# Retention without GpSimd steps, and a new order of the hybrid mixer's products, in a four-layer transformer kernel

## The chip, the core and the metric

One core of one Trainium2 chip runs the whole program. The metric is the device time of one execution in microseconds. Before the change it is 3003.79 us, the median of 3 runs (3002.36 to 3005.44).

## The reference

The input is 512 tokens of 1024 channels, in fp32. Four layers follow one another, each a mixer and a feed-forward part with residual additions: dilated attention with a short convolution, retention, and two hybrid layers. The change touches retention and the hybrid mixer, cut here to their core.

```python
def retention_mixer(xn, wq, wk, wv, wg, gn_gain, wo):      # 4 heads, q and k of 256, v of 512
    q, k, v = xn @ wq, (xn @ wk) * 256 ** -0.5, xn @ wv
    o = chunkwise_retention(rotary(q, pos), rotary(k, pos), v)
    mu, var = mean(o), mean((o - mu) ** 2)                  # over each head's 512 values
    o = (o - mu) * rsqrt(var + EPS) * gn_gain
    return (silu(xn @ wg) * o) @ wo

def hybrid_mixer(h, ...):                                   # 8 heads of 64
    q_nsa, kv_nsa, g_nsa, qkv_sb, g_merge = split(h @ w_in)
    # q is rotated; six kv parts: k and v for compressed, selected and window attention
    kc, vc = gelu(blocks(k) @ w1 + b1) @ w2, the same for v # compressed keys and values
    o_nsa = g0 * softmax(q kc) vc + g1 * softmax(q ks) vs + g2 * softmax(q kw) vw
    # stick breaking: weight of key j for query i is sigmoid(z_ij) * prod over j<l<i of (1 - sigmoid(z_il))
    g_a, g_b = split(sigmoid(g_merge))
    y = g_a * (o_nsa @ w_proj_nsa) + g_b * (o_sb @ w_proj_sb)
    return y @ w_out
```

With 512 tokens there are 8 blocks of 64 keys, and each query takes up to 16, so the selected branch sees all causal keys.

## The kernel before

All products run on TensorE in three parts (`mm3`, L161): weights and inputs are split into a rounded part and a remainder (`whi`, `wlo`; `xgh`, `xgl`), and three matmuls of them are summed. A weight unit of 512 KB is loaded by SyncE into `raw` (3 buffers), rounded by ScalarE into `whi` and subtracted by VectorE into `wlo` (4 buffers each; `unit`, L147 to L156). `lin_a` makes a product with channels on the partitions (24 matmuls of 512 columns a unit), `lin_b` one with tokens on the partitions, in four token blocks at once, and `lin_b_halves` the same by token halves: the first two blocks over all of the weights, a callback `done`, then the other two blocks. PSUM has eight banks under four names (`pa`, `psc`, `ptr`, `po`) with two buffers each.

The order that is written is a priority. The framework puts an instruction that is written later ahead of an earlier one on its engine, at build time, where it takes the earlier one to be waiting, and each engine then runs its list in order. So products that depend on little are put between the steps of a softmax. What such a product can't pass is its buffers: a `lin_a` product holds a `pa` bank until VectorE has moved it into an SBUF slot, and there are 76 slots of 128 x 512. `slot()` and `ring()` take slots from the head of a queue, and what is freed goes to its tail; a slot that is taken again is written only when its last reader is done.

Retention (`mix1`, L690): for each of four heads, `project` makes q and k and rotates them. VectorE multiplies by cosine and sine (L709, L710), GpSimd subtracts and adds (L711, L712), and `split` makes the two parts. Then come the values, the scores `weigh`, the gate, four output blocks `o` with their group norm (ScalarE writes `og`, L777; GpSimd multiplies by the gate, L778), the next head's `project`, the previous head's output product `out` (all of it in `pa` banks, added to `x` at L749), and the transposes of `og` into `gt` (L792). In the last head, `ssq_add` sums the squares of `x` on GpSimd (L297), and `ssq_col` (L305) reduces them with matmuls against a column of ones.

The hybrid mixer (`hyb`, L895) has these stages:
- **Entry.** The compressed and selected keys and values are made by `lin_b` (in the second hybrid layer, by token halves). `kv_branch` scales, rotates, packs and transposes the selected ones; then the same for the window keys (`w_in_c`) by `lin_b`; `compress` runs two small products with a gelu each; then q by `lin_b` and its rotation and transposes; then the second small products, and their results spread into `kz` and `vc` (L963 to L971); then the compressed scores and softmax (L974 to L1005).
- **Softmax stage.** For four head pairs and two branches: scores, softmax on VectorE and ScalarE (`softmax`, L487), and `finish`, which transposes the probabilities and multiplies by the values (`pv`).
- **Values and gates.** `tok_pack(w[2])` makes the stick-breaking values v and `gate` five gate tiles (`ga`, L1047).
- **Stick stage.** `heads` (L567) takes four head pairs: `prep` makes q and k of a pair by two `lin_a` products (`u`, L1065), `sticks` scores and scans (L510 to L520), and `merge_a` (L1070) multiplies a gate tile by its product; the fill list holds five of these.
- **After it.** The remaining gates, the second set of gates, and the output products.

Of the kernel before, what the change touches and what calls it, by code (L numbers as in the profile page):

```python
# [10 lines left out]
F32R = mybir.dt.float32r  # L11
# [58 lines left out]
class Kern:  # L70
# [148 lines left out]
    def lin_b_halves(self, w, xs, banks, done=None):  # L219
        cols = w.shape[2]  # L220
        per = UNIT // cols
        parts = [self.unit(w[:, k:k + per, :], UNIT) for k in range(0, KT, per)]
        outs = []
        for h in range(2):
            outs += [bank()[:, :cols] for bank in banks[2 * h:2 * h + 2]]
            for k in range(KT):
                wh, wl = parts[k // per]
                sl = slice(k % per * cols, k % per * cols + cols)
                for tb in (2 * h, 2 * h + 1):
                    tsl = slice(tb * 128, tb * 128 + 128)  # L230
# [459 lines left out]
    def mix1(self, nxt):  # L690
# [7 lines left out]
        def project(h):  # L698
            rot = []
            for w in (a["ret_wq"], a["ret_wk"]):  # L700
                t = [tmp.get(name="rt") for _ in range(4)]
                for e in range(2):
                    ps = self.lin_a(w, 2 * h + e, xs, self.pa())
                    if self.pending is not None:
                        self.norm()
                        nc.vector.tensor_tensor(cr, cr, self.rb, ALU.mult)
                        nc.vector.tensor_tensor(sr, sr, self.rb, ALU.mult)
                        self.free(self.rb)
                    nc.vector.tensor_tensor(t[2 * e], ps, cr, ALU.mult)  # L709
                    nc.vector.tensor_tensor(t[2 * e + 1], ps, sr, ALU.mult)  # L710
                nc.gpsimd.tensor_tensor(t[0], t[0], t[3], ALU.subtract)  # L711
                nc.gpsimd.tensor_tensor(t[1], t[1], t[2], ALU.add)  # L712
                rot.append([self.split(t[0], name="r0"), self.split(t[1], name="r1")])
            return rot

        def weigh(h, rot):
# [23 lines left out]
        def out(h, gt):  # L740
            nonlocal st
            for n in range(0, KT, 2):
                wh, wl = self.unit(a["ret_wo"][h, n // 2], UNIT)
                for e in range(2):
                    ps = self.pa()
                    for c in range(4):
                        sl = slice((e * 4 + c) * 128, (e * 4 + c) * 128 + 128)
                        self.mm3(ps, (wh[:, sl], wl[:, sl]), gt[c], c == 0, c == 3)
                    nc.vector.tensor_tensor(self.x[n + e], ps, self.x[n + e], ALU.add)  # L749
                    if h == 3:  # L750
                        st = self.ssq_add(st, n + e, self.x[n + e])
                        nx.append(self.xg_tile(self.x[n + e], nxt, n + e))
            self.free(gt)

        rot = project(0)
        for h in range(4):
# [7 lines left out]
            for i in range(4):  # L764
                o = self.po()
                for j in range(i + 1):
                    sl = slice((i - j) * 128, (i - j) * 128 + 128)
                    self.mm3(o, tuple(z[:, sl] for z in at[j]), v[j], j == 0, j == i)
                bn = self.sm(6, "bn")
                nc.vector.bn_stats(bn, o)  # L770
                ag = self.sm(2, "ag")
                nc.vector.bn_aggr(ag, bn)
                r = self.rstd(ag[:, 1:2], 1, 1.0)
                nb = self.sm(1, "nb")
                nc.vector.scalar_tensor_tensor(nb, ag[:, 0:1], -1.0, r, ALU.mult, ALU.mult)
                t = ro.get(name="og")
                nc.scalar.activation(t, o, AF.Identity, scale=r[:, 0:1], bias=nb[:, 0:1])  # L777
                nc.gpsimd.tensor_tensor(t, t, gs[i], ALU.mult)  # L778
                og.append(t)
            self.free(box, v, gs)  # L780
            if h < 3:
# [113 lines left out]
    def hyb(self, l, post, nxt):  # L895
# [20 lines left out]
        self.free(cmpt)  # L916


        def kv_branch(ps, name):
            ktok = [self.slot(name="kt") for _ in range(2)]  # L920
            vp = [self.slot(512, F32R, "vp") for _ in range(2)]
            for tb in range(4):
                rc = self.rc[:, tb:tb + 1]
                nc.scalar.activation(b2(ktok[tb // 2])[:, tb % 2, 0:128], ps[tb][:, 0:128], AF.Identity, scale=rc)
                self.pack(vp[tb // 2][:, tb % 2 * 256:tb % 2 * 256 + 256], ps[tb][:, 128:256], rc)
            for b in range(2):
                self.rope(b2(ktok[b])[:, :, 128:256], b2(ktok[b])[:, :, 0:128], 2 * b, 2, 2, rf)
            k = self.stack_k(self.slot, self.transp(ktok, 128), name)
            self.free(ktok)
            return k, vp  # L930

        kvs = [kv_branch([p[:, 256:512] for p in pkv], "ks")]
        ps = self.lin_b(a["w_in_c"][l], xs, [self.po, self.po, self.pa, self.pa])
        gates = self.small.tile([128, 96], F32, tag="gates", name=self.nm("gates"), bufs=1)
        for tb in range(4):
            nc.scalar.activation(gates[:, tb * 24:tb * 24 + 24], ps[tb][:, 256:280], AF.Sigmoid, scale=self.rc[:, tb:tb + 1])
        kvs.append(kv_branch(ps, "kw"))
        gk, w2k = self.compress(gbk, "ck", l)
        gv, w2v = self.compress(gbv, "cv", l)

        qt = []
        for tb, p in enumerate(self.lin_b(w[0], xs, [self.psc, self.psc, self.po, self.po])):
            raw = rf.get(name="qraw")
            nc.vector.tensor_scalar(raw, p, self.rc[:, tb:tb + 1], None, ALU.mult)
            qt.append(self.slot(name="qtok"))
            self.rope(qt[tb][:, None, :], raw[:, None, :], tb, 1, 8, rf)
        qs = [self.stack_q(self.slot, self.transp(qt, p * 128), 0.125, "q") for p in range(4)]
        self.free(qt)

        pk = self.psc()  # L950
        gv4 = rf.get(256, name="gv4")
# [12 lines left out]
        for j in range(4):  # L964
# [5 lines left out]
            r, c = slice(32 * j, 32 * j + 32), j % 2 * 256  # L970
            self.pack(vc[j // 2][r, c:c + 256], pvc[r, 0:128])  # L971

        cadd, cmul = self.table("cmp_add"), self.table("cmp_mul")
        pcT = []  # L974
        for kv in range(2):
# [5 lines left out]
                self.mm(st, kz[2 + kv][:, c], q, False, j == 3)  # L981
            sT = rf.get(name="sT")
            nc.scalar.copy(sT, st)
            s = self.ptr()
            for i in range(4):
                nc.tensor.transpose(s[:, i * 128:i * 128 + 128], sT[:, i * 128:i * 128 + 128], self.ident)
# [16 lines left out]
            for i in range(4):  # L1003
                nc.tensor.transpose(p[:, i * 128:i * 128 + 128], pc[:, i * 128:i * 128 + 128], self.ident)
            pcT.append(self.split(p, name="pcT"))  # L1005
        self.free(cadd, cmul, *kz)
        rp = self.ring(10)
        tas = [self.slot(name="ga") for _ in range(3)]
        onsa = []
        work = []  # L1010

# [13 lines left out]
        for j in range(4):  # L1025
            for b in range(2):
                ps = self.box(rp)
                for kv in range(2):
                    h = kv * 4 + j
                    self.softmax(qs[j], kvs[b][0], kv, causal, ps[kv],  # L1030
                                 gates.rearrange("p (i c) -> p i c", i=4)[:, :, h * 3 + 1 + b])
                if work:
                    finish(*work.pop())
                work.append((j, b, ps))
            self.free(qs[j])
        finish(*work.pop())
# [1 line left out]
        rp.close(), rt.close(), rc.close()  # L1038

        rf.close()  # L1040
        wm = a["w_in_a"][l]
        self.first_stick = None
        self.tok_pack(w[2], [self.pa, self.pa], v)

        def gate(g, n):
            ps = self.lin_a(wm, n, xs, self.pa())
            nc.vector.tensor_tensor(g, ps, self.rb, ALU.mult)  # L1047
# [22 lines left out]
        def merge_a(n):  # L1070
# [4 lines left out]
        ready = len(tas)  # L1075
        osb = self.heads(prep, lambda c, e, ps: self.sticks(c[0], c[1], e, ps, tmp),
                         v, rp, rt, rc, [lambda n=n: merge_a(n) for n in range(ready)])
        rp.close(), rt.close(), rq.close(), tmp.close(), ru.close(), rc.close()

        for n in range(ready, KT):  # L1080
            tas.append(self.slot(name="ga"))
            gate(tas[n], 8 + n)
            merge_a(n)
        self.free(onsa)
        gbs = []
        for n in range(KT):
            gbs.append(self.slot(name="gb"))
            gate(gbs[n], 16 + n)
            sigmoid(gbs[n])
        self.free(self.xs, self.rb)  # L1090
        ys = []
# [177 lines left out]
```

## Time and profile before

| | us |
|---|---|
| median of 3 runs | 3003.79 |
| profiled execution, its own time | 3006.11 |
| its span, from the first to the last instruction | 3004.4 |
| outside the span | 1.7 |
| TensorE matmuls busy | 2938.6 (98%) |
| VectorE busy | 1898.5 (63%) |
| ScalarE busy | 1362.9 (45%) |
| GpSimd busy | 280.8 (9%) |
| mean granted TensorE clock | 0.995 |

TensorE is busy for nearly all of the span, so the table is read by what is missing: 65.8 us in which no matmul ran, and the stretches in which the granted clock was at its lower level. Stages are read from windows of the trace, and what ended a wait from the view of waits.

### The profile page before, as it was taken

The numbers are of one execution on the slowest core, as the hardware profiler recorded it, in microseconds if no ns is written. First come the engines' busy times: TensorE is split into PE (matmuls) and PEld (weight loads), VectorE is DVE, ScalarE is ACT, GpSimd is POOL, SyncE is SP. The second block draws the span as 40 slices with busy tenths as digits, with TensorE's granted clock in tenths as the row PEclk, the third lists the DMA queues.
The fourth block names the chain that finished last, engine by engine and source line by source line (L and its number), as shares of the span: only waits on it lengthen the run. The fifth ranks groups of instructions, "written<-read, shape, count | busy, mean of one in ns | idle before, by whom it ended". The sixth has DMA issues, their size and how long they took to land.

```text
span 3004.4 us, 36799 instructions
## 1 busy us (share of the span) xinstructions
PE 2938.6 (98%) x14060; PEld 2432.1 (81%) x14060; DVE 1898.5 (63%) x3084; ACT 1362.9 (45%) x2268; POOL 280.8 (9%) x303
## 2 busy tenths in 40 slices
PE   8999999999999999999999999999999999999998
PEld 7788888888888788888787788888877878888887
DVE  6876774344544677535888648774279884587732
ACT  4834443333333444324567435443356673454432
POOL 1010000111110100011003011000120040110000
PEclk9999999999999999999999999999999999999999
DMA  4033333322222233333101332323241113333332
GB/s 160 29 107 97 99 96 92 111 88 83 82 87 80 89 96 95 99 116 126 45 32 53 104 107 85 98 93 96 90 142 43 36 53 102 99 99 98 96 92 73
DMA packets 83937, 267.91 MB, mean 89 GB/s; under 512 B 9776, under 2 KB 12464, under 8 KB 83760
## 3 DMA queue, kind: packets, MB, share of 16 engines
q1 hardware_dynamic: 83760, 265.55, 28.0%
q8 instruction: 111, 1.82, 0.2%
q14 instruction: 66, 0.54, 0.1%
HBM read 258.17 MB, written 6.29 MB: 88 GB/s over the span
## 4 chain that ended last, share of the span: by engine, by line
PE 87%; DVE 7%; ACT 3%; issue 1%; POOL 0%; DMA 0%; SPq 0%; DVEq 0%; ACTq 0%; POOLq 0%
PE pa L159 38%; PE psc L159 21%; PE po L159 15%; PE ptr L159 11%; PE ptr L536 1%; DVE om L519 1%; DVE xgl L271 1%; DVE p L520 1%; DVE ptl L268 0%; ACT p L496 0%; DVE wlo L155 0%; ACT whi L154 0%; DVE x L409 0%; DVE m L408 0%; DVE rp L847 0%
## 5 line engine op out<-in xcount | busy, mean ns | idle before, releaser
L155 DVE TENSOR_TENSOR wlo<-raw,whi 128x1024 fp32r<-128x1024 f32 (+3 forms) x497 | 587.6, 1184 | 484.2 <-ACT whi L154 479.9
L154 ACT CAST whi<-raw 128x1024 fp32r<-128x1024 f32 (+2 forms) x491 | 494.5, 1008 | 871.8 <-PE pa L159 354.9
L159 PE MATMUL pa<-xgh,whi 128*128 128x512 f32 (+1 forms) x1344 | 519.4, 386 | 0.0
L159 PE MATMUL pa<-xgl,whi 128*128 128x512 f32 (+1 forms) x1344 | 519.4, 386 | 0.0
L159 PE MATMUL pa<-xgh,wlo 128*128 128x512 f32 (+1 forms) x1344 | 519.1, 386 | 0.0
L297 POOL TENSOR_TENSOR acc<-acc,sq 128x512 f32<-128x512 f32 (+1 forms) x99 | 131.2, 1326 | 1747.3 <-ACT sq L295 1746.1
L159 PEld LDWEIGHTS pa<-xgh,whi 128*128 128x128 f32 x1344 | 252.9, 188 | 47.1 <-DVE rt L710 0.2
L159 PEld LDWEIGHTS pa<-xgh,wlo 128*128 128x128 f32 x1344 | 252.8, 188 | 46.7
L159 PEld LDWEIGHTS pa<-xgl,whi 128*128 128x128 f32 x1344 | 252.8, 188 | 46.2
L159 PE MATMUL psc<-xgl,whi 128*128 128x512 f32 x672 | 261.8, 390 | 1.0 <-DVE xgl L271 1.0
L159 PE MATMUL psc<-xgh,whi 128*128 128x512 f32 x672 | 262.0, 390 | 0.3 <-ACT xgh L270 0.3
L159 PE MATMUL psc<-xgh,wlo 128*128 128x512 f32 x672 | 261.3, 389 | 0.0
L267 ACT CAST hh<-y 128x512 fp32r<-128x512 f32 x88 | 54.6, 620 | 222.2 <-DVE y L370 222.2
L159 PEld LDWEIGHTS psc<-xgl,whi 128*128 128x128 f32 x672 | 126.2, 188 | 27.2 <-DVE xgl L271 1.3
L159 PEld LDWEIGHTS psc<-xgh,whi 128*128 128x128 f32 x672 | 126.2, 188 | 26.6 <-ACT xgh L270 0.7
L159 PEld LDWEIGHTS psc<-xgh,wlo 128*128 128x128 f32 x672 | 126.2, 188 | 26.1
L159 PE MATMUL ptr<-hh,whi 128*128 128x512 f32 x352 | 136.9, 389 | 0.0
L159 PE MATMUL ptr<-hl,whi 128*128 128x512 f32 x352 | 136.9, 389 | 0.0
L159 PE MATMUL ptr<-hh,wlo 128*128 128x512 f32 x352 | 136.9, 389 | 0.0
L344 DVE SCALAR_TENSOR_TENSOR y<-u,cols,y 128x510 f32<-128x510 f32 x176 | 131.7, 749 | 5.7
L343 DVE SCALAR_TENSOR_TENSOR y<-u,cols,y 128x511 f32<-128x511 f32 x176 | 131.1, 745 | 4.6 <-ACT y L340 4.1
L159 PE MATMUL po<-hh,wlo 128*128 128x512 f32 (+1 forms) x352 | 132.3, 376 | 0.0
(399 smaller groups left out, 5771.9 us busy)
## 6 DMA issues: line engine op xcount, KB each, us to landing
raw<-ffn_w_up SPq DMA_DIRECT2D x88, 512.0 KB, 3.5
raw<-w_up SPq DMA_DIRECT2D x88, 512.0 KB, 3.5
raw<-w_in_a SPq DMA_DIRECT2D x48, 512.0 KB, 3.5
raw<-ffn_w_down SPq DMA_DIRECT2D x32, 512.0 KB, 3.5
raw<-w_down SPq DMA_DIRECT2D x32, 512.0 KB, 3.5
raw<-w_in_b SPq DMA_DIRECT2D x24, 512.0 KB, 3.4
raw<-ret_wv SPq DMA_DIRECT2D x16, 512.0 KB, 3.4
raw<-ret_wg SPq DMA_DIRECT2D x16, 512.0 KB, 3.4
```

What stands on the lines that cost most here:

```text
L154: (nc.vector.tensor_copy if step < n else nc.scalar.copy)(hi[:, cs], raw[:, cs])
L155: nc.vector.tensor_tensor(lo[:, cs], raw[:, cs], hi[:, cs].bitcast(F32), ALU.subtract)
L159: self.nc.tensor.matmul(out, l, r, start=start, stop=stop)
L267: nc.scalar.copy(hi, src)
L271: nc.vector.scalar_tensor_tensor(lo, src, scale, hi.bitcast(F32), ALU.mult, ALU.subtract)
L297: nc.gpsimd.tensor_tensor(st["sum"][0][:, hs], st["sum"][0][:, hs], sq[:, hs], ALU.add)
L343: nc.vector.scalar_tensor_tensor(y[:, 1:T], u[:, 0:T - 1], self.col(w, i * 3 + 1), y[:, 1:T], ALU.mult, ALU.add)
L344: nc.vector.scalar_tensor_tensor(y[:, 2:T], u[:, 0:T - 2], self.col(w, i * 3), y[:, 2:T], ALU.mult, ALU.add)
L519: nc.vector.tensor_tensor_scan(r, r, r, 1.0, ALU.mult, ALU.min)
L520: nc.vector.tensor_tensor(be[:, :n - 1], be[:, :n - 1], om[:, 1:n], ALU.mult)
L536: nc.tensor.transpose(t[:, c:c + 128], ps[e][i][:, j * 128:j * 128 + 128], self.ident)
```

## The change

In retention, the rotation's subtract and add go to VectorE, each followed by its split. In `out`, every other product goes to a `psc` bank. The squares of the last two tiles of `x` are no longer added on GpSimd, but are reduced by `ssq_col` as tiles of their own. The group norm scales the gate by 1/sd on ScalarE and forms (o - mean) * gate on VectorE, from PSUM, in one step.

In the hybrid mixer, the window keys and q are made by token halves; the transposes of the selected keys move behind both gelus and those of the window keys behind the compressed scores; q moves behind `kz` and `vc`; gate tiles 8, 9 and 10 are made in the entry (behind the gelus, behind q, and inside the compressed scores). `finish` comes after the first of two softmaxes of a step. The values v and gates 11 and 12 become the first fill of the stick stage, behind the first stick scores, and the fifth merge moves behind that stage.

```diff
@@ lin_b_halves
-        parts = [self.unit(w[:, k:k + per, :], UNIT) for k in range(0, KT, per)]
+        parts = [self.unit(w[:, k:min(k + per, KT), :], min(per, KT - k) * cols) for k in range(0, KT, per)]
@@ mix1: project
-                nc.gpsimd.tensor_tensor(t[0], t[0], t[3], ALU.subtract)
-                nc.gpsimd.tensor_tensor(t[1], t[1], t[2], ALU.add)
-                rot.append([self.split(t[0], name="r0"), self.split(t[1], name="r1")])
+                r = []
+                for e, op in enumerate((ALU.subtract, ALU.add)):
+                    nc.vector.tensor_tensor(t[e], t[e], t[3 - e], op)
+                    r.append(self.split(t[e], name=f"r{e}"))
+                rot.append(r)
@@ mix1: out
-                    ps = self.pa()
+                    ps = (self.pa, self.psc)[e]()
-                        st = self.ssq_add(st, n + e, self.x[n + e])
+                        st = self.ssq_add(st, n + e, self.x[n + e], 2)
@@ mix1: group norm
-                nb = self.sm(1, "nb")
-                nc.vector.scalar_tensor_tensor(nb, ag[:, 0:1], -1.0, r, ALU.mult, ALU.mult)
-                nc.scalar.activation(t, o, AF.Identity, scale=r[:, 0:1], bias=nb[:, 0:1])
-                nc.gpsimd.tensor_tensor(t, t, gs[i], ALU.mult)
+                nc.scalar.activation(gs[i], gs[i], AF.Identity, scale=r[:, 0:1])
+                nc.vector.scalar_tensor_tensor(t, o, ag[:, 0:1], gs[i], ALU.subtract, ALU.mult)
@@ hyb: entry
-        kvs = [kv_branch([p[:, 256:512] for p in pkv], "ks")]
-        ps = self.lin_b(a["w_in_c"][l], xs, [self.po, self.po, self.pa, self.pa])
+        for h in range(2):
+            kv_branch(0, h, [p[:, 256:512] for p in pkv[2 * h:2 * h + 2]])
+        def kw_done(h, ps):
+            kv_branch(1, h, ps)
+            for tb, p in enumerate(ps, 2 * h):
+                nc.scalar.activation(gates[:, tb * 24:tb * 24 + 24], p[:, 256:280], AF.Sigmoid, scale=self.rc[:, tb:tb + 1])
+        self.lin_b_halves(a["w_in_c"][l], xs, [self.po, self.po, self.pa, self.pa], kw_done)
         gk, w2k = self.compress(gbk, "ck", l)
         gv, w2v = self.compress(gbv, "cv", l)
-        qt = []
-        for tb, p in enumerate(self.lin_b(w[0], xs, [self.psc, self.psc, self.po, self.po])):
...
+        kvs = [kv_stack(0, "ks")]
+        tas = []
+        def gate(n):
+            g = self.slot(name="ga" if n < 16 else "gb")
+            ps = self.lin_a(wm, n, xs, self.pa())
+            nc.vector.tensor_tensor(g, ps, self.rb, ALU.mult)
+            return g
+        tas.append(gate(8))
...
+        self.lin_b_halves(w[0], xs, [self.psc, self.psc, self.po, self.po], q_done)
+        tas.append(gate(9))
+        qs = [self.stack_q(self.slot, self.transp(qt, p * 128), 0.125, "q") for p in range(4)]
...
             nc.scalar.copy(sT, st)
+            if kv == 0:
+                tas.append(gate(10))
...
+        kvs.append(kv_stack(1, "kw"))
         rp = self.ring(10)
-        tas = [self.slot(name="ga") for _ in range(3)]
@@ hyb: softmax stage
...
-                if work:
-                    finish(*work.pop())
+                    if work:
+                        finish(*work.pop())
@@ hyb: values, gates, sticks
-        self.tok_pack(w[2], [self.pa, self.pa], v)
-        tas.extend(self.slot(name="ga") for _ in range(2))
-        for n, g in enumerate(tas):
-            gate(g, 8 + n)
+        def values():
+            self.tok_pack(w[2], [self.pa, self.pa], v)
+            tas.extend(gate(n) for n in (11, 12))
-                         v, rp, rt, rc, [lambda n=n: merge_a(n) for n in range(ready)])
+                         v, rp, rt, rc, [values] + [lambda n=n: merge_a(n) for n in range(ready - 1)])
         rp.close(), rt.close(), rq.close(), tmp.close(), ru.close(), rc.close()
+        merge_a(ready - 1)
```

## Rows read from the trace of the kernel before

**Rows 1.** The page, part 1: engine, busy us, share of the span, instructions

```profile
PE 2938.6 (98%) x14060; PEld 2432.1 (81%) x14060; DVE 1898.5 (63%) x3084; ACT 1362.9 (45%) x2268; POOL 280.8 (9%) x303
```

**Rows 2.** Windows: stretch, length, PE, PEld, DVE, ACT, POOL busy, PEclk, DMA, GB/s

```profile
1389.00:1459.00 70.00, 64.69 (x378) 54.06 (x378) 49.87 (x119) 35.53 (x75) 11.04 (x15) 0.95 0.30 93
1459.00:1571.00 112.00, 109.61 (x611) 88.61 (x610) 100.48 (x305) 78.41 (x204) 2.60 (x2) 1.00 0.11 36
1571.00:1594.00 23.00, 23.00 (x107) 19.17 (x107) 14.01 (x20) 11.44 (x18) 0.00 (x0) 1.00 0.25 81
1594.00:1677.00 83.00, 75.49 (x375) 57.86 (x373) 76.90 (x125) 60.41 (x130) 32.72 (x64) 1.00 0.20 61
2203.00:2273.00 70.00, 63.49 (x385) 52.78 (x384) 50.70 (x118) 35.63 (x75) 12.00 (x15) 1.00 0.33 106
```

**Rows 3.** Waits of TensorE in retention, 600 to 1012 us: total us, times, longest

```profile
PE pa L159 <- DVE x L749: 2.7, 4, 1.0
PE ptr L792 <- DVE gtl L271: 2.5, 2, 1.9
PE psc L159 <- DVE xgl L271: 1.0, 1, 1.0
```

**Rows 4.** Windows in retention's first head

```profile
690.00:700.00 10.00, 8.09 (x42) 6.52 (x41) 7.05 (x8) 3.47 (x5) 3.52 (x2) 1.00 0.32 105
700.00:710.00 10.00, 10.00 (x42) 8.20 (x41) 2.99 (x4) 2.74 (x4) 0.00 (x0) 0.83 0.16 54
```

**Rows 5.** Groups of GpSimd in retention: count, busy us, mean ns, idle before

```profile
L778 POOL TENSOR_TENSOR og<-og,g 128x512 f32<-128x512 f32 x16 | 20.5, 1295 | 262.2 <-ACT og L777 185.0 <-PE pa L159 74.3 <-issue 2.9
L711 POOL TENSOR_TENSOR rt<-rt,rt 128x512 f32<-128x512 f32 x8 | 18.2, 2270 | 0.0
```

**Rows 6.** Groups of VectorE in retention: two subtractions of one form, 128x512

```profile
L268 DVE TENSOR_TENSOR r1l<-rt,r1h 128x512 fp32r<-128x512 f32 x6 | 10.6, 1773 | 0.0
L268 DVE TENSOR_TENSOR r0l<-rt,r0h 128x512 fp32r<-128x512 f32 x6 | 4.2, 692 | 0.8
```

**Rows 7.** Timeline of TensorE at retention's end: start us, us, instruction, count

```profile
1011.43 0.95 PE L159 MATMUL ptr<-one,acc 128*128 128x1 f32 x8
```

**Rows 8.** Waits of TensorE in the first hybrid entry, 1389 to 1458 us

```profile
PE psc L159 <- DVE vc L268: 3.2, 1, 3.2
PE ptr L447 <- POOL kt L845: 0.9, 1, 0.9
```

**Rows 9.** Timeline of TensorE behind the long wait of that entry

```profile
1452.15 5.46 PE L159 MATMUL psc<-q,kz 128*128 128x512 f32 x12 [3.15 <-DVE vc L268]
```

**Rows 10.** Waits of TensorE at the second hybrid layer's first product, 2178 to 2190

```profile
PE psc L159 <- DVE wlo L155: 0.7, 2, 0.4
```

**Rows 11.** Groups of VectorE in the first softmax stage that serve other products

```profile
L155 DVE TENSOR_TENSOR wlo<-raw,whi 128x1024 fp32r<-128x1024 f32 x8 | 9.8, 1219 | 0.0
L1047 DVE TENSOR_TENSOR ga<-pa,rb 128x512 f32<-128x512 f32 x4 | 2.7, 676 | 0.0
L271 DVE SCALAR_TENSOR_TENSOR vp<-pa,rc,vp 128x256 fp32r<-128x256 f32 x4 | 1.9, 471 | 0.0
```

**Rows 12.** Timeline of VectorE behind that stage: results of two neighbouring lin_a products

```profile
1577.07 0.69 DVE L1065 TENSOR_TENSOR u<-pa,rb 128x512 f32<-128x512 f32 x1 [1.40 <-PE pa L159]
1582.51 0.69 DVE L1065 TENSOR_TENSOR u<-pa,rb 128x512 f32<-128x512 f32 x1 [2.64 <-PE pa L159]
```

**Rows 13.** A window of the softmax stage between two filler products

```profile
1485.00:1490.00 5.00, 3.98 (x27) 3.44 (x28) 4.91 (x16) 3.31 (x10) 0.00 (x0) 1.00 0.01 3
```

**Rows 14.** Waits of TensorE in the first half of the stick stage

```profile
PE psc L159 <- ACT om L512: 3.5, 4, 1.5
PE po L159 <- DVE ptl L268: 0.9, 2, 0.7
```

**Rows 15.** A window of the stick stage

```profile
1615.00:1625.00 10.00, 7.32 (x35) 5.06 (x33) 9.69 (x18) 8.92 (x21) 4.92 (x10) 1.00 0.25 79
```

More of the change, by code (lines that the diff above doesn't have):

```diff
@@ L916, in hyb, with kv_branch @@
         self.free(cmpt)
[L919 to L922, printed above, removed]
+        ktok = [[self.slot(name="kt") for _ in range(2)] for _ in range(2)]
+        vps = [[self.slot(512, F32R, "vp") for _ in range(2)] for _ in range(2)]
+        def kv_branch(i, h, ps):
+            for tb, p in enumerate(ps, 2 * h):
                 rc = self.rc[:, tb:tb + 1]
[L924 to L930, printed above, removed]
@@ L932, in hyb @@
-        kvs = [kv_branch([p[:, 256:512] for p in pkv], "ks")]
-        ps = self.lin_b(a["w_in_c"][l], xs, [self.po, self.po, self.pa, self.pa])
-        gates = self.small.tile([128, 96], F32, tag="gates", name=self.nm("gates"), bufs=1)
-        for tb in range(4):
-            nc.scalar.activation(gates[:, tb * 24:tb * 24 + 24], ps[tb][:, 256:280], AF.Sigmoid, scale=self.rc[:, tb:tb + 1])
-        kvs.append(kv_branch(ps, "kw"))
+                nc.scalar.activation(b2(ktok[i][h])[:, tb % 2, 0:128], p[:, 0:128], AF.Identity, scale=rc)
@@ new lines, in kv_branch, with kv_stack @@
+                self.pack(vps[i][h][:, tb % 2 * 256:tb % 2 * 256 + 256], p[:, 128:256], rc)
+            self.rope(b2(ktok[i][h])[:, :, 128:256], b2(ktok[i][h])[:, :, 0:128], 2 * h, 2, 2, rf)
+        def kv_stack(i, name):
+            k = self.stack_k(self.slot, self.transp(ktok[i], 128), name)
+            self.free(ktok[i])
+            return k, vps[i]
+        for h in range(2):
+            kv_branch(0, h, [p[:, 256:512] for p in pkv[2 * h:2 * h + 2]])
+        gates = self.small.tile([128, 96], F32, tag="gates", name=self.nm("gates"), bufs=1)
@@ L938, in hyb @@
+        def kw_done(h, ps):
+            kv_branch(1, h, ps)
+            for tb, p in enumerate(ps, 2 * h):
+                nc.scalar.activation(gates[:, tb * 24:tb * 24 + 24], p[:, 256:280], AF.Sigmoid, scale=self.rc[:, tb:tb + 1])
+        self.lin_b_halves(a["w_in_c"][l], xs, [self.po, self.po, self.pa, self.pa], kw_done)
         gk, w2k = self.compress(gbk, "ck", l)
         gv, w2v = self.compress(gbv, "cv", l)
-        qt = []
-        for tb, p in enumerate(self.lin_b(w[0], xs, [self.psc, self.psc, self.po, self.po])):
[L943 to L946, printed above, removed]
@@ L947, in hyb @@
-        qs = [self.stack_q(self.slot, self.transp(qt, p * 128), 0.125, "q") for p in range(4)]
-        self.free(qt)
+        kvs = [kv_stack(0, "ks")]
+        wm = a["w_in_a"][l]
+        tas = []
[5 more added lines that the diff above has]
+        tas.append(gate(8))
         pk = self.psc()
@@ L971, in hyb, with q_done @@
             self.pack(vc[j // 2][r, c:c + 256], pvc[r, 0:128])
+        qt = []
+        def q_done(h, ps):
+            for tb, p in enumerate(ps, 2 * h):
+                raw = rf.get(name="qraw")
+                nc.vector.tensor_scalar(raw, p, self.rc[:, tb:tb + 1], None, ALU.mult)
+                qt.append(self.slot(name="qtok"))
+                self.rope(qt[tb][:, None, :], raw[:, None, :], tb, 1, 8, rf)
+        self.lin_b_halves(w[0], xs, [self.psc, self.psc, self.po, self.po], q_done)
+        tas.append(gate(9))
+        qs = [self.stack_q(self.slot, self.transp(qt, p * 128), 0.125, "q") for p in range(4)]
+        self.free(qt)
         cadd, cmul = self.table("cmp_add"), self.table("cmp_mul")
@@ L1040, in hyb @@
         rf.close()
-        wm = a["w_in_a"][l]
         self.first_stick = None
-        self.tok_pack(w[2], [self.pa, self.pa], v)
-        def gate(g, n):
-            ps = self.lin_a(wm, n, xs, self.pa())
-            nc.vector.tensor_tensor(g, ps, self.rb, ALU.mult)
         def sigmoid(g):
@@ L1073, in merge_a @@
             nc.vector.tensor_tensor(tas[n], ps, tas[n], ALU.mult)
-        ready = len(tas)
+        def values():
+            self.tok_pack(w[2], [self.pa, self.pa], v)
+            tas.extend(gate(n) for n in (11, 12))
+        ready = 5
         osb = self.heads(prep, lambda c, e, ps: self.sticks(c[0], c[1], e, ps, tmp),
-                         v, rp, rt, rc, [lambda n=n: merge_a(n) for n in range(ready)])
+                         v, rp, rt, rc, [values] + [lambda n=n: merge_a(n) for n in range(ready - 1)])
         rp.close(), rt.close(), rq.close(), tmp.close(), ru.close(), rc.close()
+        merge_a(ready - 1)
         for n in range(ready, KT):
-            tas.append(self.slot(name="ga"))
-            gate(tas[n], 8 + n)
+            tas.append(gate(8 + n))
             merge_a(n)
@@ L1086, in hyb @@
         for n in range(KT):
-            gbs.append(self.slot(name="gb"))
-            gate(gbs[n], 16 + n)
+            gbs.append(gate(16 + n))
             sigmoid(gbs[n])
```

## The prediction

> **What bounds the kernel.** I read the page's first part, then windows by stage, then the waits of each stage, then single instructions. TensorE is busy for 98% of the span [rows 1], and the change neither adds nor removes products, so it can gain only what TensorE loses now: idle time between matmuls, and matmuls run at the lower of its two clock levels. In the stretches that the change touches this is about 7 us in retention [rows 3, 4]; in the first hybrid layer 5.3 us in the entry, 2.4 in the softmax stage and 7.5 in the stick stage, and in the second layer's entry 6.5 (length less busy) [rows 2]. The second layer's other stages repeat the first's within 0.2 us. The reader should also see who is short of time beside TensorE: VectorE is busy for 100.5 of 112 us in the softmax stage and 76.9 of 83 in the stick stage, but for 14.0 of 23 between them and 49.9 of 70 in the entry [rows 2]. So the change moves TensorE work (gates, v) between stages in which VectorE is the second bound. The profiled execution took 3006.1 us, 2.3 above the median; a difference of 0.2%, or 6.0 us, is about what a measurement of this kernel can tell from no change.
>
> **Retention.** Four waits for `x`, 2.7 us, are for one of the two `pa` banks [rows 3]. With products alternating between `pa` and `psc` a bank is needed again only four products later: minus 2.7. Two waits for `gtl` cost 2.5 us, the long one 1.9 in the first head [rows 3, 4], and behind it the granted clock is 0.83 over 10 us, that is 3.4 us at 1.2 GHz, or 1.7 lost [rows 4]. Before it stands the rotation: GpSimd takes 2.27 us for one subtraction, and VectorE's `r1l` beside it 1.77 where the same form, `r0l`, takes 0.69 [rows 5, 6]. On VectorE the two combining steps cost 2 x 0.69, so the chain gets little shorter, but nothing is stretched. Of the 1.9 + 1.7 I take half: minus 1.8 (ends 0 and 3.6). At the end one wait for `xgl`, 1.0 us [rows 3], should go, as the last square sums no longer run beside it: minus 1.0. Against it, `ssq_col` reduces three tiles in place of one; eight of its records take 0.95 us on TensorE [rows 7], so two more sets cost plus 1.9. The group norm replaces a GpSimd step of 1.30 us [rows 5] by a VectorE step from PSUM; the nearest row for VectorE is 0.69, and the next head's projection stands behind it on TensorE. VectorE gains 16 + 16 such steps, some 22 us over four heads, but is busy for only 7.05 of 10 us even around the long wait [rows 4]. I cost both at nothing; if that cover failed, they would cost one such wait per head, 1 us each. Sum: **minus 3.6**.
>
> **Entry.** The longest wait, 3.2 us, is for `vc`: the spreading of the compressed keys holds both `psc` banks while the filler has run out [rows 8]. The twelve matmuls behind it take 5.46 us [rows 9], where 24 matmuls of that width take 5.44 (two neighbouring results are that far apart [rows 12]), so 2.7 us are lost at 1.2 GHz. In the second layer this stage shows a granted clock of 1.00 [rows 2], so nothing of that kind is there. The change puts q behind that spreading, with its second token half on `po` banks, and three gates of 5.44 us into the entry, where half of v (48 matmuls, 10.9 us) stood. The rotated keys' wait of 0.9 [rows 8] goes behind the gelus. I leave 0.9 us per layer, for the compressed softmax. First layer 5.3 - 0.9 + 2.7, second 6.5 - 0.9: **minus 12.7** (ends 0 and minus 14.5). The four weight units of q are now wanted within one half, 10.9 us; the one place that already works so shows 0.7 us of waits for `wlo` [rows 10], which I keep in the range, not in the sum. Weights, SyncE's loads and their number are the same, in another order: where six units fall together, with v and two gates behind the first sticks, they are wanted at one per 5.4 us, as between the stages now (81 GB/s [rows 2]).
>
> **Softmax stage.** This is the price. Now half of v and five gates (168 matmuls at 0.227 us, 38.1 us) fill it. Without them TensorE's own work is 109.6 - 38.1 = 71.5 us, and VectorE's 100.5 less `wlo`, `ga` and `vp` (9.8 + 2.7 + 1.9) [rows 11] = 86.1. What follows in the new order are the first `prep` products. By the queue of slots their results (`u`) take slots of the ring that the last `pv` of this stage still writes, so only two can run ahead, filling both `pa` banks and stopping every product behind them, v too. So TensorE has 71.5 + 10.9 = 82.4 us of work, and VectorE 86.1 + 4 x 1.22 for weights = 91.0. If VectorE is never idle, TensorE waits 8.6 us, against 2.4 now: plus 6.2, and 0.7 for moving the first `u` at the stage's end. For two layers **plus 13.8**. Ends: plus 2, if VectorE does part of this under the entry; plus 33, if the two products are used up in the entry and TensorE idles as in a slice with no filler, busy for 3.98 of 5 us [rows 13]: 71.5 / 0.796 = 89.8, so 18.3 idle, less 2.4, plus 0.7, twice.
>
> A rule speaks against this step by the clock. In the slice of the stick stage with most waits TensorE is busy for 7.32 of 10 us and its granted clock stays 1.00 [rows 15], so I give the clock no term. The Trainium skill (TensorE: Matmul & The Clock Gate, section on psum-queue depth-cycling) says that brief idling between groups of matmuls can make the clock go back and forth; by it the sum would lie higher, and the trace does not agree so far.
>
> **Stick stage.** The waits of its first half, 3.5 + 0.9 us [rows 14], come while the first sticks pile up on VectorE. With v and two gates behind the first scores (32.7 us of TensorE work, some 16 of VectorE's), VectorE has caught up before the next. I take 3.6 of 4.4 per layer: **minus 7.2** (ends 0 and minus 8.8). The later waits stay; the fifth merge behind the stage only moves. The new place of `finish` changes the order, not the work: nothing, as VectorE's sum bounds that stage either way.
>
> **The sum** is -3.6 - 12.7 + 13.8 - 7.2 = -9.7 us: 2996.4 against the profiled execution, 2994 against the median.
>
> **Rivals.**
> 1. Forecast, 2994 us, chance 0.36.
> 2. The starved stage costs next to nothing (plus 2 for both layers): -21.5, 2982 us. For it: VectorE has 20 us to spare in the entry. Against: the softmax steps can't start before q. Chance 0.16.
> 3. Slower: the softmax stage is starved in full, plus 33 and the other terms as forecast, +9.5, 3013 us. It decides where TensorE idles over 14 us there per layer (break-even); over 17 it is slower by 0.2%. For it: the slice without filler [rows 13]. Against: two products should be left for it. Chance 0.23.
> 4. The entry is not filled: q's halves wait for weights or for the banks as `vc` did, and that term is 0: +3.0, 3007 us, no change that can be told. Chance 0.18.
> 5. The clock falls in the starved stage. One fall costs 1.7 us [rows 4]; one per head pair, four a layer, gives +13.6 on the forecast: 3008 us. For it: both falls above came with a wait of 1.9 us or more. Against: rows 15. Chance 0.07. The rule of the skill above is this rival.
>
> **How the numbers follow.** Cases 1 and 2 lie under 2997.8 us, but case 1 only by 4 us, so 0.05 of it goes to no change: faster 0.47, same 0.05 + 0.18 + 0.07 = 0.30, slower 0.23. The range runs from case 2, with 2 us for a retention chain that goes entirely, to nearly case 3: 2980 to 3012. In this range the softmax stage's bounds and the 0.7 us waits for weights are held.
>
> **What would show it.** Right: no wait for `x` at the output product and none for `vc`; the granted clock 1.00 through the entry; v's `vp` steps behind the first `om`; the softmax stage near 95 us with VectorE busy for over 95% of it and TensorE idle for 8 to 10 us; two `u` moved right at its end. Wrong: a softmax stage as long as 112 us or with TensorE busy throughout (v ran ahead after all), waits for `wlo` of more than 1 us in the entry, or clock falls in the softmax stage.

## The result and the profile after

The changed kernel takes **3042.65 us** (median of 3 runs, 3042.16 to 3045.01) against 3003.79: ratio 1.0127, 95% interval 1.0112 to 1.0141, slower. The forecast was 2994 us, with a range from 2980 to 3012. Sign and size are wrong.

The page of the changed kernel, part 1 (columns as in [rows 1]), span 3040.4 us:

```profile
PE 2961.8 (97%) x14076; PEld 2439.2 (80%) x14076; DVE 1901.6 (63%) x3100; ACT 1364.3 (45%) x2270; POOL 227.4 (7%) x269
```

TensorE shows 23.2 us more busy time than in [rows 1], with 16 small matmuls more; 12.8 us more are idle. The span is cut below at marks that every trace has: a mixer and a feed-forward part each begin at their first `ptr<-one,acc`, the sums of squares of their input; in a hybrid layer the softmax stage runs from the first score `psc<-ks,q` to the first stick score `psc<-sk,sq`, the stick stage and the rest to the start of the feed-forward part. Before, after, and what the terms of the prediction make of each:

| stretch, us | before | after | change | forecast |
|---|---|---|---|---|
| retention | 413.0 | 403.6 | -9.4 | -5.5 |
| the feed-forward part behind it | 377.2 | 380.6 | +3.4 | +1.9 |
| hybrid 1: entry | 70.5 | 75.0 | +4.5 | -1.7 |
| softmax stage | 134.1 | 119.0 | -15.1 | -31.2 |
| stick stage and the rest | 209.1 | 241.1 | +32.0 | +29.1 |
| hybrid 2: entry, with what stands before | 101.7 | 107.3 | +5.6 | -0.2 |
| softmax stage | 133.8 | 119.0 | -14.8 | -31.2 |
| stick stage and the rest | 209.1 | 241.1 | +32.0 | +29.1 |

(The forecast's column counts the moved work: entry, three gates of 5.44 in and half of v, 10.9, out; softmax stage, 38.1 out and 6.9 of idle time in; stick stage, 32.7 in and 3.6 of waits out. The softmax stage between these marks takes in the 23 us that [rows 2] show between the stages.) The other stretches are 2.2 us shorter together. The two hybrid layers are 44.2 us longer where 6.1 less was forecast: 32.5 of that difference lie in the softmax stages, 12.0 in the entries, 5.8 in the stick stages and what follows.

**Retention** went as reasoned around its long wait: TensorE is full where [rows 4] show 8.09 of 10 us and a clock of 0.83. But the waits at its end have not gone, and a fall of the clock now stands behind them. Windows, columns as in [rows 2]:

```profile
690.00:700.00 10.00, 10.00 (x54) 8.21 (x53) 7.46 (x11) 5.44 (x8) 0.00 (x0) 1.00 0.19 58
700.00:710.00 10.00, 10.00 (x46) 8.29 (x45) 2.45 (x2) 1.37 (x2) 0.00 (x0) 1.00 0.51 150
1000.00:1010.00 10.00, 9.71 (x52) 8.43 (x52) 2.40 (x4) 1.97 (x4) 0.00 (x0) 0.83 0.33 107
```

TensorE's timeline there, before and then after, columns as in [rows 7]: the waits are 0.69 and 0.29 us where they were 0.29 and 0.97, and the 16 matmuls of the two more square sums take 1.93 us where 1.9 was reckoned.

```profile
1009.38 0.50 PE L159 MATMUL psc<-xgh,whi 128*128 128x512 f32 x1 [0.29 <-ACT xgh L270]
1010.85 0.50 PE L159 MATMUL psc<-xgl,whi 128*128 128x512 f32 x1 [0.97 <-DVE xgl L271]
```

```profile
999.57 0.49 PE L159 MATMUL psc<-xgh,whi 128*128 128x512 f32 x1 [0.69 <-ACT xgh L270]
1000.36 0.50 PE L159 MATMUL psc<-xgl,whi 128*128 128x512 f32 x1 [0.29 <-DVE xgl L271]
...
1001.75 1.93 PE L159 MATMUL ptr<-one,sq 128*128 128x1 f32 x16
```

**The first hybrid layer** by windows: entry, the stage's first 19 us, its middle, its end, the stick stage.

```profile
1382.00:1457.00 75.00, 69.27 (x400) 58.63 (x400) 51.24 (x119) 36.97 (x72) 12.03 (x10) 0.95 0.33 100
1457.00:1476.00 19.00, 17.83 (x87) 13.34 (x86) 15.95 (x39) 9.93 (x22) 2.59 (x2) 1.00 0.17 56
1476.00:1564.00 88.00, 76.21 (x404) 55.39 (x405) 76.00 (x256) 62.50 (x176) 0.00 (x0) 1.00 0.02 7
1564.00:1576.00 12.00, 12.00 (x58) 10.08 (x58) 9.77 (x15) 8.75 (x14) 0.00 (x0) 1.00 0.11 34
1576.00:1670.00 94.00, 90.79 (x430) 71.58 (x429) 71.13 (x113) 60.97 (x129) 26.19 (x60) 1.00 0.19 58
```

For 88 us hardly a weight comes from memory (7 GB/s): nothing runs but the stage's own work. TensorE shows 76.21 us busy, yet its weight loads (PEld in the rows, a step of TensorE itself and no transfer) only 55.39, where the filled stage has 88.6 of 112 [rows 2]. Busy time counts a lone matmul for more: in the timelines here a 128x512 matmul behind a wait shows 0.47 to 0.50 us, while one in a row adds 0.23 (24 in 5.44 us [rows 12]). The Trainium skill (Perfetto Trace Analysis, section on identifying the most-contended engine) says that matmul busy time is no good measure of how close a kernel is to its roofline, as pipelined instructions look smaller in the trace, and goes by the weight loads' busy time. VectorE isn't full either, 76.00 of 88.

In the entry two waits stand where [rows 8] have those for `vc` and `kt`. Waits of TensorE, 1382 to 1457 us, columns as in [rows 3]:

```profile
PE ptr L447 <- POOL qtok L845: 3.0, 2, 2.4
PE psc L159 <- DVE vc L268: 2.3, 1, 2.3
```

The timeline shows the clock fall behind each: from 1417.27 and 1445.37 on, a 128x512 matmul takes 0.61 to 0.63 us.

```profile
1416.04 0.47 PE L159 MATMUL psc<-whi,xgh 128*128 128x512 f32 x1 [2.31 <-DVE vc L268]
...
1417.27 0.61 PE L159 MATMUL psc<-whi,xgl 128*128 128x512 f32 x1
...
1442.77 0.66 PE L447 MATMUL ptr<-ident,qtok 128*128 128x128 f32 x4 [2.43 <-POOL qtok L845]
...
1445.37 0.63 PE L159 MATMUL pa<-xgh,whi 128*128 128x512 f32 x1
```

### The profile page after: what moved, and what is told of

Same layout as the page of the kernel before. It is cut to its first block, busy times and chain, and to the rows that moved or that the text cites. A ratio compares the mean times of both kernels' runs of the same rounds, so it can differ in the third digit from the quotient of the medians.

```text
span 3040.4 us, 36814 instructions
## 1 busy us (share of the span) xinstructions
PE 2961.8 (97%) x14076; PEld 2439.2 (80%) x14076; DVE 1901.6 (63%) x3100; ACT 1364.3 (45%) x2270; POOL 227.4 (7%) x269
## 5 line engine op out<-in xcount | busy, mean ns | idle before, releaser
L155 DVE TENSOR_TENSOR wlo<-raw,whi 128x1024 fp32r<-128x1024 f32 (+3 forms) x497 | 581.4, 1171 | 489.7 <-ACT whi L154 485.0
```

Of the source, the lines that this page charges most:

```text
L155: nc.vector.tensor_tensor(lo[:, cs], raw[:, cs], hi[:, cs].bitcast(F32), ALU.subtract)
```

## The experiments

Each kernel was timed beside the kernel before on the same chip (3005.5 to 3005.9 us there); ratios are to that. The first five take the change apart.

**Retention alone** (e1_ret), on the kernel before.

```diff
- nc.gpsimd.tensor_tensor(t[0], t[0], t[3], ALU.subtract)
- nc.gpsimd.tensor_tensor(t[1], t[1], t[2], ALU.add)
...
+ nc.vector.tensor_tensor(t[e], t[e], t[3 - e], op)
+ r.append(self.split(t[e], name=f"r{e}"))
...
- ps = self.pa()
+ ps = (self.pa, self.psc)[e]()
...
- st = self.ssq_add(st, n + e, self.x[n + e])
+ st = self.ssq_add(st, n + e, self.x[n + e], 2)
...
- nc.gpsimd.tensor_tensor(t, t, gs[i], ALU.mult)
+ nc.scalar.activation(gs[i], gs[i], AF.Identity, scale=r[:, 0:1])
+ nc.vector.scalar_tensor_tensor(t, o, ag[:, 0:1], gs[i], ALU.subtract, ALU.mult)
```

> The kernel before with the four retention edits alone. All theories: the traces of before and after put retention at 413.0 and 403.6 us, and the feed-forward part behind it at 377.2 and 380.6, so 9.4 less and 3.4 more: about 2998 us. If the retention edits also changed something in the hybrid layers, by another order of the slots, the time would lie off that by more than 3 us.

Measured: 3000.80, ratio 0.9982 (0.9972 to 0.9991): faster by some 5 us.

**The same without the larger square sums** (e6_ret_no_tail).

```diff
- st = self.ssq_add(st, n + e, self.x[n + e], 2)
+ st = self.ssq_add(st, n + e, self.x[n + e])
```

> The kernel before with three of the four retention edits: the rotation on VectorE, the output products on pa and psc in turn, the group norm on VectorE; the square sums stay as before (all added on GpSimd). In e1_ret, with all four, the retention stage is 9.3 us shorter, but the head of the layer behind it 3 to 5 us longer. Theory T (the two more square-sum tiles cost that: eight matmuls of 0.95 us a set, 1.9, and a clock fall behind it): that head goes back to 377.2 us, and the total is 2 to 5 us under e1_ret, 2996 to 2999. Rival: the last sum on GpSimd is late when the residual is, so the wait for xgl of 1.0 us is back and the head keeps most of its length; the total is e1_ret's 3000.8 within 1.5 us.

Measured: 3000.67, ratio 0.9984 (0.9975 to 0.9994). Retention and the part behind it come to 783.9 us in the profile, against 786.0 with all four edits, but the medians agree: the rival. The two waits there are 1.15 and 1.03 us, against 0.70 and 0.29 with all four and 0.29 and 0.97 in the kernel before, and a clock fall stands behind them too. The larger square sums gain nothing that the medians can tell.

**Values and two gates alone** (e2_values), on the kernel before: from behind the softmax stage into the fill list of `heads`, as in the change; gates 8 to 10 stay where they were.

```diff
- self.tok_pack(w[2], [self.pa, self.pa], v)
...
+ def values():
+     self.tok_pack(w[2], [self.pa, self.pa], v)
+     for n in (3, 4):
+         tas.append(self.slot(name="ga"))
+         gate(tas[n], 8 + n)
...
```

> The kernel before, with v and the gates 11 and 12 moved behind the first sticks and nothing else; gates 8 to 10 stay behind the softmax stage. Theory S (the softmax stage starves): its filler falls from about 38 us of TensorE work to the 16 of three gates and the first two products of prep, so each hybrid layer gets 8 to 16 us longer, 3020 to 3036 us in all, and VectorE stays under 90% busy there. Rival E (the new entry order is what costs, the move of v is harmless): 3002 to 3006 us. Rival F (the new place of finish costs): 3002 to 3006 us.

Measured: 3040.72, ratio 1.0117 (1.01 to 1.0134). This one part costs 34.9 us, nearly all of the change's 38.9; it is worse than even theory S had it.

**The change without that part** (e3_v_back): v and the two gates stand behind the softmax stage again, five merges in the fill list.

```diff
  self.first_stick = None
+ self.tok_pack(w[2], [self.pa, self.pa], v)
+ tas.extend(gate(n) for n in (11, 12))
...
- def values():
-     self.tok_pack(w[2], [self.pa, self.pa], v)
-     tas.extend(gate(n) for n in (11, 12))
...
```

> The changed kernel, with v and the gates 11 and 12 moved back to their old place behind the softmax stage and nothing else undone. Theory S: the softmax stage has 33 us of filler again and at least 15 us per layer come back, so 3042 falls to 3000 to 3012 us. Rival E: 3036 to 3043 us. Rival F: 3036 to 3043 us.

Measured: 3008.48, ratio 1.001 (1.0 to 1.0019): 34.2 us come back. Against retention alone (3000.8) the new entry costs 7.7 us where it was to gain 12.7. Between the marks its entries take 74.6 and 107.6 us, as in the change (75.0 and 107.3).

**The place of finish alone** (e4_finish), on the kernel before: into the loop over `kv`.

```diff
-                 if work:
-                     finish(*work.pop())
+                     if work:
+                         finish(*work.pop())
```

> The kernel before, with finish behind the first of the two softmaxes of a step and nothing else. Theory S and rival E: 3002 to 3006 us. Rival F (one finish between two softmaxes delays the second and lengthens the stage): 3012 us or more.

Measured: 3004.05, ratio 0.9995 (0.9986 to 1.0005). Nothing, as forecast.

**q's halves with the banks the other way round** (e5_q_on_po), on the change without the moved values.

```diff
- self.lin_b_halves(w[0], xs, [self.psc, self.psc, self.po, self.po], q_done)
+ self.lin_b_halves(w[0], xs, [self.po, self.po, self.psc, self.psc], q_done)
```

> The kernel of e3_v_back (the change, with v and gates 11 and 12 back behind the softmax stage) with one edit: q's first token half takes the two po banks and its second half the two psc banks, the other way round than in the change. Theory B (the entry of the change loses time because q's first half waits for the psc banks that the spreading of the compressed keys holds, 2.3 us each layer, with a granted clock of one half for 3.4 us behind it, 1.7 lost): both go, and the time falls from e3's 3008.5 us by up to 2 x 4.0 us, to 3000.5 to 3004. Theory G (the wait for GpSimd's part of the rotation of q sets the entry, so a start of q that comes earlier ends at the same place): the wait for vc goes, the wait for qtok grows from 2.4 + 0.6 us by as much, and the time stays within 2 us of 3008.5.

Measured: **2994.14**, ratio 0.9962 (0.9949 to 0.9975): 14.3 us less, nearly twice what theory B had at most (8.0). The wait for `vc` goes and that for `qtok` falls from 3.0 to 0.8 us, as the waits of TensorE from 1384 to 1451 us show, and the entry's window has no clock fall:

```profile
PE ptr L447 <- POOL qtok L845: 0.8, 2, 0.5
PE pa L159 <- ACT gates L942: 0.4, 1, 0.4
```

```profile
1384.00:1451.00 67.00, 65.82 (x401) 56.73 (x402) 51.51 (x119) 36.92 (x72) 11.18 (x10) 1.00 0.37 112
```

The first half of q runs while the compressed keys are spread (1410.66 to 1421.67 us), so its rotation is done early, and the second half covers most of what was the wait for `qtok`, which theory B left out. The entries take 67.0 and 99.4 us. The order of two bank names was worth 7 us a layer.

**No early gates**: gates 8 to 10 go from the entry to behind the softmax stage, with the banks as in the change (e7_halves_only), and the other way round (e11_po_halves).

```diff
- tas.append(gate(8))
...
- tas.append(gate(9))
...
- tas.append(gate(10))
...
- tas.extend(gate(n) for n in (11, 12))
+ tas.extend(gate(n) for n in range(8, 13))
```

> The kernel of e3_v_back with gates 8, 9 and 10 put back behind the softmax stage too, so that of the change in the hybrid layers there is left: q and the window keys in token halves, and the new order of the key stacks; nothing new fills the entry. Theory E (early gates in the entry are used up before the waits, and the softmax stage misses them as filler): the softmax stage gains some 3 us a layer, the entry loses as filler some 3 to 5 us, and the total is 3006 to 3012. Theory F (the three gates are of use in neither place, the entry's loss is from the halves): 3008.5 within 2 us. Rival: without the gates the entry has no filler at all, and the two waits (vc, qtok) grow by most of a gate's 5.4 us each: 3020 or more.

Measured: 3012.55, ratio 1.0025 (1.0016 to 1.0034), 4.1 above the kernel with the gates; a little over theory E's upper end.

> The kernel of e7_halves_only (no gate in the entry) with q's halves on the po banks first, as in e5_q_on_po. Theory B (the order of the banks is what cost the entry its time): it falls from e7's 3012.6 us by 12 to 16 us, as e5 did from e3, to 2996 to 3001. Theory BG (early gates are needed too, since with nothing else in the entry TensorE meets the waits for the compressed keys' softmax): it falls by less than 8 us, to 3005 or more.

Measured: 3007.73, ratio 1.0011 (1.0001 to 1.002): theory BG. Banks and early gates work together: the three gates are worth 4.1 us with the change's banks, 13.6 with the swapped ones. Without the gates TensorE waits 5.1 us at the transposes of the compressed keys' probabilities (L1024; the row names the VectorE step that ended at the same time as theirs) and 2.0 for a gelu (waits of this kernel, 1384 to 1600 us):

```profile
PE ptr L1024 <- DVE rd L497: 5.1, 1, 5.1
PE psc L159 <- ACT gh L888: 2.0, 1, 2.0
```

**A part of the moved work** (e12_two_gates_late). On the kernel with the swapped banks, gates 11 and 12 go behind the first sticks, first in the fill list; v doesn't.

```diff
  self.tok_pack(w[2], [self.pa, self.pa], v)
- tas.extend(gate(n) for n in (11, 12))
...
+ def values():
+     tas.extend(gate(n) for n in (11, 12))
...
```

> The kernel of e5_q_on_po, but gates 11 and 12 (10.9 us a layer of the 32.7 that the change moves) go behind the first sticks, as in the change; v stays behind the softmax stage. Moving all 32.7 costs 17 us a layer (the changed kernel against e3_v_back). Theory P (each piece of filler taken from the softmax stage costs its share): 10.9 of 32.7 of 17 us, 5.7 a layer, 3005.5 us. Theory K (the stage has a floor, and costs begin only below it; the three gates that e5 takes away from it against e11_po_halves cost nothing): with the first 10.9 us still above the floor the time is 2994 within 3 us, and v's 21.8 us cost all of the 17. Rival: with less filler in the softmax stage but more behind the first sticks, where the waits of 1.1 and 1.5 us are, there is a gain: under 2991.

Measured: 3004.28, ratio 0.9997 (0.9987 to 1.0006), 10.1 above the kernel with the swapped banks: theory P, neither theory K nor the gain of its rival. The softmax stage loses 10.9 us of work and gets 5.2 shorter (134.3 to 129.1, first layer).

**Slots for u** (e8_u_slots). In the changed kernel a `prep` product's result gets free slots before the softmax stage.

```diff
  rp = self.ring(10)
+ rf.close()
+ ru = self.ring(2)
...
- rf.close()
- rq, ru, rc = self.ring(12), self.ring(2), self.ring(2)
+ rq, rc = self.ring(12), self.ring(2)
```

> The changed kernel with one edit: the ring rf is given back before the softmax stage, not behind it, and the ring ru (two slots, for u) is taken there, so that the result of a prep product need not wait for slots that the last pv of the softmax stage still writes. The stage's own work is unchanged. Theory S1 (the softmax stage is starved because both prep products have run in the entry and nothing behind them may start while their u wait for slots): with slots free, two more products (10.9 us) and their successors fill the stage, and the time falls by 8 to 11 us a layer, to 3020 to 3027. Rival S2 (the stage is bound by VectorE or by its own chain, so other filler finds no room, or what it fills is missing later): 3042.6 within 4 us.

Measured: 3032.62, ratio 1.0088 (1.0071 to 1.0105), 10.0 us less: the direction of S1, half its size. S1 has both products run in the entry; the trace of the changed kernel has them in the stage's first 19 us, from 1456.80 to 1475.58. There VectorE moves the two `u` only when the stage's last `ptl` is done, so no product starts behind them from 1476 to 1564 us; its timeline:

```profile
1562.99 0.69 DVE L268 TENSOR_TENSOR ptl<-ptr,pth 128x512 fp32r<-128x512 f32 x1 [1.26 <-ACT pth L267]
1563.78 1.29 DVE L1081 TENSOR_TENSOR u<-pa,rb 128x512 f32<-128x512 f32 x2
```

With the edit the first `u` moves at 1468.88, two more products run (1476.5 to 1507.8), and the stage is starved again: its length falls from 119.0 to 111.1, while the stick stage up to its last score grows by 2.8.

**Less VectorE work** in the softmax of the changed kernel (e9_scale_on_act), and of the one with swapped banks (e10_po_scale_act).

```diff
+ if gate is not None and i == 3:
+     nc.scalar.activation(p, p, AF.Identity, scale=rd[:, i:i + 1])
+ else:
      nc.vector.tensor_scalar(p, p, rd[:, i:i + 1], None, ALU.mult)
```

> The changed kernel with one edit: in the softmax of the hybrid layers the largest of the four scalings of p by rd (128x512, 0.48 us on VectorE, 16 a layer) goes to ScalarE. In the starved stage of the changed kernel VectorE is busy for 88% of each 22 us and ScalarE for 74%. Theory V (VectorE's own work is the floor under the stage): 7.7 us less of it, and the time falls by 5 to 8 us a layer, to 3027 to 3033. Rival L (the chain of small steps between TensorE, ScalarE and VectorE is the floor, 12% of VectorE's time being waits in it): ScalarE's steps become longer or more, and the time stays within 4 us of 3042.6, or rises.

Measured: 3037.35, ratio 1.0106 (1.0091 to 1.0121), 5.3 us less: between the two theories. The stage falls from 119.0 to 114.9, by about half of the 7.7 us. Windows of the middle of the stage, changed kernel and then this one:

```profile
1503.00:1525.00 22.00, 19.79 (x107) 14.65 (x107) 19.41 (x70) 16.24 (x47) 0.00 (x0) 1.00 0.01 1
1525.00:1547.00 22.00, 19.64 (x107) 14.62 (x107) 19.40 (x69) 16.17 (x47) 0.00 (x0) 1.00 0.00 1
```

```profile
1503.00:1525.00 22.00, 20.18 (x112) 15.15 (x111) 19.15 (x67) 19.36 (x55) 0.00 (x0) 1.00 0.01 1
```

VectorE stays near 87%, and ScalarE is as busy now. The stage got half as much shorter as VectorE's work did, which fits neither theory alone; how VectorE's sum and the chain share the length stays open.

> The kernel of e5_q_on_po with the edit of e9_scale_on_act. There the stage is filled with half of v and two gates. Theory V: VectorE's 7.7 us less a layer shorten this stage too, as far as TensorE is idle in it or its matmuls wait; at most 2 to 4 us a layer, to 2986 to 2991. Rival: filled, the stage is bound by TensorE, and the time stays within 2 us of 2994.

Measured: **2991.98**, ratio 0.9952 (0.9936 to 0.9969), the fastest here. It is 2.2 us under the kernel with swapped banks, between what theory and rival said, and the softmax stages are 2.0 and 1.2 us shorter; the medians alone could hardly tell the two apart.

## Why the prediction was wrong

**Softmax stage, the step that failed: "If VectorE is never idle".** VectorE's work was right: 15.95 + 76.00 = 91.95 us from 1457 us until the two `u` move at 1564, where the forecast has 91.0 and makes that the length. But the stretch takes 107 us: VectorE is busy for 86% of it. Between the marks the stage takes 119.0 us, against the forecast's 102.9 (134.1 - 31.2). VectorE waits in the chain of each softmax; its waits in the changed kernel, 1481 to 1547 us:

```profile
DVE rd L497 <- ACT p L496: 4.8, 6, 0.9
DVE ptl L268 <- ACT pth L267: 1.4, 5, 0.3
DVE p L494 <- PE psc L159: 0.6, 1, 0.6
```

That is 6.8 of 66 us, and it hardly gets better with filler: in the kernel with v put back the best filled window has VectorE at 20.25 of 22 (the mean of four is 19.93), and TensorE's weight loads at 18.45 in place of 14.6:

```profile
1529.00:1551.00 22.00, 21.97 (x126) 18.45 (x125) 20.25 (x62) 16.23 (x45) 0.00 (x0) 1.00 0.13 37
```

So no single engine's sum sets the stage's length: of 32.7 us of TensorE work taken from it, it gives back 14.6 (133.6 to 119.0, first layer), of the first 10.9 us 5.2. I took TensorE's busy share for its load; with 2.4 us listed as idle I thought the stage nearly full, where the filler partly ran in time that the stage took anyway. The 82.4 us of TensorE work in the forecast failed with it: that stretch shows 17.83 + 76.21 = 94.0 us busy.

**"Two products should be left for it"**, the argument against rival 3. They were left: only the three gates run in the entry, and the two products start with the stage and are done by 1476 us, 19 us into it. Their `u` then wait for slots, as the queue of slots said. So the stage starved without the condition that rival 3 set, and by more than its price: its upper end (18.3 us idle per layer from [rows 13]) took the busy share of one 5 us slice and priced 33 us for both layers; measured against the forecast's 102.9, the stage is 16.1 us longer per layer on top of the 6.9 that was in the sum, 46 for both. Nor would its sign have told: TensorE shows 107 - 94.0 = 13 us idle there, less than the 14 that it gives as break-even.

**Stick stage, "I take 3.6 of 4.4 per layer".** The waits for `om` did fall, from 3.5 us [rows 14] to 1.2 in the whole stick stage, but stage and rest are 32.0 us longer for 32.7 moved: 0.7 gained. Where the rest of the 2.3 us went is not shown. v and the two gates run while the other engines have little to do (window of the changed kernel):

```profile
1599.00:1621.00 22.00, 22.00 (x101) 18.10 (x100) 10.87 (x16) 9.05 (x16) 1.91 (x4) 1.00 0.27 84
```

TensorE is full and VectorE half idle. There moved work costs its full length; in the softmax stage it had cost half. That difference, 17 us a layer, is the loss. The price is not the same everywhere. With the banks swapped, putting three gates (16.3 us) into the entry moves 34 of v's 96 matmuls (7.7 us), which had filled it, on into the softmax stage: for 8.6 us of work net the entry gets 5.0 us longer (62.0 to 67.0, first layer; 8.0 in the second) and the softmax stage 12.6 shorter (146.9 to 134.3), where the waits for the compressed keys' probabilities fall from 6.1 to 1.4 us.

**Entry, "first layer 5.3 - 0.9 + 2.7".** The prediction put q's second half on `po` and overlooked that the first half needs the `psc` banks that the spreading holds. That is rival 4, "for the banks as `vc` did", which I priced as no gain at all. With the wait for `qtok`, which I did not see coming, and two clock falls the entries got 4.5 and 5.6 us longer, 6.2 and 5.8 more than forecast. With the banks swapped they take 67.0 and 99.4 us, where the forecast makes 68.8 and 101.5: the term was right for another kernel than this one.

**Retention: mechanism right except at the end, size low.** I took half of the wait for `gtl` and of its clock fall; all of it went, 4.2 us where 1.8 was reckoned (2.5 of waits and 1.7 at the lower clock), and the 2.7 for `x` as forecast. The 1.0 us at the end did not come: 0.98 us of waits are left of 1.26. That makes 7.2 of the 9.4 us by which retention is shorter, where 5.5 was forecast without the square sums; the other 2.2 are not traced to a wait. Behind it came 1.5 more than the reckoned 1.9, with a new clock fall at 1004 us. Alone it measured 5 us, of 3.6 forecast. The new place of `finish`: nothing, right.

**The clock in the starved stage: no term, right for this kernel.** Its granted clock is 1.00 throughout, with TensorE idle in small pieces for 12 of 88 us. The Trainium skill (TensorE: Matmul & The Clock Gate, section on psum-queue depth-cycling) tells of a kernel in which brief idling between groups of matmuls made the clock go back and forth; this stage does not show it. The kernel with values and two gates alone shows one fall there in each layer, the first behind a wait of 1.60 us.

## What to carry to other kernels

Before moving filler out of a stage, ask what the stage takes without it: read the weight loads' busy time and the waits inside each engine's chain there, not TensorE's busy share, and test with a small piece: per microsecond of work its price was nearly the large one's (5.0 of 10.9, 17 of 32.7). Put filler where TensorE would otherwise wait in a chain with the other engines; where it is full and they have little to do, filler costs its full length. Give the first half of a split product the banks that are free first. If a product may run ahead, see that its result has somewhere to go.

## What the hardware showed that was not expected

- TensorE's clock fell to 1.2 GHz for 3.4 us behind waits of 2.3 and 2.4 us in the changed kernel's entry, with TensorE full before them. In the kernel with swapped banks it also fell behind a wait of 1.11 us that ended at 1472 us, and not behind the wait of 1.5 us for `om` that ended at 1610 us. In the changed kernel the same wait of 1.11 us, at 1478 us, has no fall behind it. So the length of the last wait alone doesn't tell. Windows of the kernel with swapped banks, columns as in [rows 2]:

```profile
1475.00:1485.00 10.00, 9.25 (x50) 7.53 (x49) 8.04 (x24) 7.14 (x21) 0.00 (x0) 0.86 0.01 2
1605.00:1615.00 10.00, 7.31 (x34) 5.08 (x33) 9.69 (x16) 7.77 (x17) 5.69 (x11) 1.00 0.27 79
```

- VectorE's `r1l` takes 0.68 us with GpSimd's subtractions gone, against 1.77 beside them [rows 6] (group of VectorE in the changed kernel's retention):

```profile
L268 DVE TENSOR_TENSOR r1l<-rt,r1h 128x512 fp32r<-128x512 f32 x8 | 5.5, 682 | 0.0
```
